# Zero-padded rows for the decay, rate and index products of a streaming encoder layer, whole modulation units, and a later load of constants

## The chip, the cores and the metric

The kernel runs on one core of one Trainium2 chip. The metric is device time in microseconds. Before the change it was 1761.67 us, the median of three runs (1757.67, 1761.67, 1761.89).

## The reference

One layer of a hybrid encoder for two groups of requests with the same weights: a prompt of 256 tokens, and 8 sample sequences of 16 tokens each with 256 cached tokens. The width is 1024.

```python
mod = silu(c) @ w_ada + b_ada                 # 6 x 1024 per sequence: shift1, scale1, gate1, shift2, scale2, gate2
h = rmsnorm(x) * (1 + scale1) + shift1
P = h @ w_in                                  # RWKV columns | attention and indexer | two branch gates
# branch A: RWKV-7 time mixing, 16 heads of 64
X = P + (P_prev - P) * mu                     # token shift; split r, k, v, wd (64), ad (64), gd
decay = exp(-exp(-softplus(-(w0 + tanh(wd) @ w_up)) - 0.5))
a = sigmoid(a0 + ad @ a_up)                   # rate
...                                           # state update per token, group norm, bonus, gate
# branch B: sparse attention, 16 heads of 64
score[t, s] = sum_h w[t, h] * relu(q_idx[t, h] . k_idx[s])     # 8 index heads of 64
...                                           # keep the best min(256, L/4) keys, softmax attention over them
m = sigmoid(gA) * (oA @ w_proj_a) + sigmoid(gB) * (oB @ w_proj_b)
x = x + gate1 * (m @ w_out)
x = x + gate2 * peer(rmsnorm(x) * (1 + scale2) + shift2)       # product-key mixture of 16384 experts
```

The outputs are the two results, the RWKV states, the last shifted rows and the new keys, values and index keys.

## The kernel before, in words

All 384 tokens (128 sample, 256 prompt) are handled together. A framework plans the program: it takes the instructions in the order in which the Python code makes them as their priority, simulates the engines, and lays down for each engine and for the SP queue (SyncE, which issues nearly all DMAs) a fixed order with waits. So engines work their queue in order, and a later edit can move instructions that it does not name. Memory comes from pools; a new tile waits until the tiles whose place it takes have been read for the last time.

`run` (L1590) has these stages:

- The front (to about 57 us): constants, the normalised input, the modulation units 0 to 7 that the first normalisation needs, and `rwkv_head` (L515), which makes the token-shifted low-rank inputs. `self.XW` holds 64 rows of decay input (after tanh) and 64 rows of rate input in one tile.
- The body (to about 692 us) works through `ORDER` (L177), one letter a unit: R is a pair of RWKV heads (`rwkv_pair`, L535), I the indexer (`index`, L890), the digits 1 to 3 the selection of keys, D a quarter of the attention (`dsa_quarter`, L932), G a gate unit, M a modulation unit from number 8 on (`mod_unit`, L383). Most of TensorE's work is three single-pass products of split (hi and lo) operands for each weight; weights arrive as 512 KB pieces through `raw` (L236), a ring of four buffers.
- The mix (`mix`, L1175) projects both branches, then the output projection, the expert scores, and the experts, which last to the end.

All products go through `mm` (L224). One on fewer than 128 rows (partitions of the operands) uses a part of the array; two on different row halves can be in it together. The places that matter here:

- `rwkv_pair`, L559 to L562: per pair of heads, the decay product takes rows 0 to 63 of `wup` and `XW`, the rate product rows 64 to 127, each of 384 columns.
- `index` (L912 to L930) makes the transposed indexer queries, `qiTs` for the sample (64 rows) and `qiTp` for the prompt (two heads one above the other, 64 rows each). `index_s` (L1015) multiplies them with the cached index keys `cki` (L1034, 64 rows of 256 columns, loaded by SP) and the new keys `kiT`; `index_p` (L983) multiplies one row half at a time. ACT applies the relu, and PE (sample) or DVE (prompt) adds up the heads.
- `mod_unit`: eight products of 32 output rows in four column groups of the array, four for each 512 KB half of the weight.
- `load_consts("clate", ...)`, L336: 200 KB of constants, used at L1203 and L1274 in the mix stage and by the experts' selection.

Of the kernel before, what the change touches and what calls it, by code (L numbers as in the profile page):

```python
# [17 lines left out]
AF = mybir.ActivationFunctionType  # L18
# [9 lines left out]
NT = 384  # L28
# [92 lines left out]
def layout(inp):  # L121
    f = {k: np.asarray(v) for k, v in inp.items()}
    A = {}

    def chunks(v):
        return v.reshape(-1, 128).T

    A["x"] = np.concatenate([f["x_sample"].reshape(128, 1024), f["x_prompt"].reshape(256, 1024)], 0)
    cc = np.concatenate([f["c_sample"], f["c_prompt"]], 0)
    A["cT"] = cc.T.reshape(8, 128, 9).transpose(1, 0, 2)  # L130
    A["w_ada"] = units256(f["w_ada"][0])
    A["b_ada"] = f["b_ada"]
    A["b_col"] = chunks(f["b_ada"][0, :2048])
    mu = np.zeros((27 * 128,), np.float32)
    mu[:RW] = f["mu_rw"][0]

    mu[RW:RW + 64] = np.tile(f["mu_rw"][0, RW - 32:], 2)
    sh = np.zeros((8, 27 * 128), np.float32)
    sh[:, :RW] = f["state_shift"][0]
    sh[:, RW:RW + 64] = np.tile(f["state_shift"][0, :, RW - 32:], 2)  # L140
    A["cols"] = np.concatenate([chunks(f["norm1_w"][0]), chunks(mu), chunks(f["w0"][0]), chunks(f["a0"][0]),
                                chunks(f["k_k"][0]), chunks(f["k_a"][0]), chunks(f["r_k"][0].reshape(-1)),
                                chunks(f["b_gate"][0])], 1)
    A["shT"] = sh.reshape(8, 27, 128).transpose(2, 0, 1)
    A["rows"] = np.concatenate([f["norm2_w"][0], f["lnx_w"][0], f["lnx_b"][0], f["b_gate"][0],
                                f["q_norm_w"][0], f["k_norm_w"][0]])[None]
    w3 = f["w_in"][0].reshape(8, 128, -1).transpose(1, 0, 2)
    A["w_in"] = np.concatenate([(np.tile(w3[:, :, c:c + 32], 3) if n == "wg" else w3[:, :, c:c + w]).reshape(128, -1)
                                for n, (c, w) in UNITS.items()], 1)
    A["wup2"] = np.concatenate([f["w_up"][0], f["a_up"][0]], 0)  # L150
    A["gup"] = np.concatenate([f["g_up"][0]] + 2 * [f["g_up"][0, 128:]], 0)
    for n in ("w_proj_a", "w_proj_b", "w_out", "w_pq"):
        A[n] = units256(f[n][0])
    A["keysT"] = f["peer_keys"][0].transpose(1, 3, 0, 2).reshape(128, 8, 128)
    A["puv"] = np.concatenate([f["peer_u"][0], f["peer_v"][0]], 1)
    A["pv"] = f["peer_v"][0]

    A["puT"] = f["peer_u"][0].reshape(128, 128, 8, 128).transpose(0, 3, 2, 1)

    A["cKT"] = f["cache_k"][0].reshape(4, 2, 256, 4, 2, 2, 64).transpose(3, 0, 5, 6, 1, 4, 2).reshape(4, 4, 128, 2, 2, 256)  # L160
    A["cV"] = f["cache_v"][0].reshape(4, 2, 2, 128, 4, 256).transpose(4, 0, 3, 1, 2, 5)
    A["cKI"] = f["cache_kidx"][0].transpose(2, 0, 1)
    A["S0"] = f["state_wkv"][0].reshape(8, 8, 2, 64, 64).transpose(2, 4, 1, 0, 3).reshape(128, 8, 8, 64)
    for n, (a, _) in PACKS.items():
        A[n] = a
    return {k: np.ascontiguousarray(v) for k, v in A.items()}
# [29 lines left out]
class K:  # L196
# [132 lines left out]
    def setup_front(self):  # L329
        nc = self.nc  # L330
        self.expb = self.fconst.tile([128, 8, 4, 16], BF16, name="expb")
        nc.vector.tensor_tensor(self.expb, self.c["blk"].unsqueeze(2).unsqueeze(3).to_broadcast([128, 8, 4, 16]),
                                self.c["dtt"].unsqueeze(1).unsqueeze(1).to_broadcast([128, 8, 4, 16]), op=OP.mult)
        rn = self.t([128, 128], tag="qkn")
        nc.sync.dma_start(rn, self.I["rows"][:, 5120:5248].to_broadcast([128, 128]))
        self.load_consts("clate", self.const)  # L336

        self.rt = self.fconst.tile([128, 3, 3, 4, 32], F32, name="rt")
        self.load_consts("crope", self.pool)
        rope = self.c["rope"]  # L340
        cos, sin = rope[:, :, 0], rope[:, :, 1]
        r = self.rt[:, 0]
        nc.gpsimd.tensor_copy(r[:, :, 0], cos)
        nc.gpsimd.tensor_copy(r[:, :, 1], cos)
        nc.gpsimd.tensor_scalar(r[:, :, 2], sin, -1.0, None, op0=OP.mult)
        nc.gpsimd.tensor_copy(r[:, :, 3], sin)
        for j in range(2):
            w1 = rn[:, 64 * j:64 * j + 32].unsqueeze(1).to_broadcast([128, 3, 32])
            w2 = rn[:, 64 * j + 32:64 * j + 64].unsqueeze(1).to_broadcast([128, 3, 32])
            r = self.rt[:, 1 + j]  # L350
            for m, w in enumerate((w1, w2, w2, w1)):
                nc.gpsimd.tensor_tensor(r[:, :, m], self.rt[:, 0, :, m], w, op=OP.mult)
        self.i64 = self.fconst.tile([128, 64], F32, name="i64")
        nc.vector.tensor_tensor(self.i64, self.ident[:, 0:64], self.ident[:, 64:128], op=OP.add)

        z = self.t([128, 520], tag="zero")
        nc.gpsimd.memset(z, 0.0)
        self.Bs, self.Bp, self.Bn = [], [], []
        for _ in range(2):
            b = self.dt_([64, 516])  # L360
            nc.sync.dma_start(b, z[:64, :516])
            self.Bs.append(b)
            for q in (self.Bp, self.Bn):
                b = self.dt_([64, 520])
                nc.sync.dma_start(b, z[:64])
                q.append(b)
# [16 lines left out]
    def mod_unit(self, u):  # L383

        nc = self.nc
        p = self.ps([128, 256], tag="mm")
        for h in range(2):
            w = self.raw(self.I["w_ada"][:, u, h * 4:h * 4 + 4])
            for g in range(4):
                self.mm(p[32 * g:32 * g + 32], self.st[:, h * 4 + g], w[:, g], start=(h == 0), stop=(h == 1), tp=(0, 32 * g))  # L390
        mr = self.t([128, 256], tag="mr", bufs=2, pool=self.fill)
        nc.scalar.activation(mr, p, AF.Copy)
        if u < 8:
            q = self.ps([128, 2, 9], tag="bx")
# [120 lines left out]
    def rwkv_head(self):  # L515
        nc = self.nc
# [5 lines left out]
        self.XW = self.shifted("wa", 24, "XW", 1)  # L522
        xv = self.shifted("wb", 25, "sig", 1)
        xg = self.shifted("wg", 26, "ra", 1)
        nc.scalar.activation(self.XW[0:64], self.XW[0:64], AF.Tanh)
        self.sigmoid(xv, xv)
        self.sigmoid(xg[:96], xg[:96])
        self.XV = [self.t([128, NT], F32R, tag=tag) for tag in ("XVh", "XVl")]
# [6 lines left out]
    def rwkv_pair(self, e):  # L535

        nc = self.nc
# [8 lines left out]
        wup = self.t([128, 128], tag="wup")  # L546
# [9 lines left out]
        nc.scalar.activation(gh[:96, 1], gup[:96, 1], AF.Copy)  # L556
        nc.vector.tensor_tensor(gh[64:96, 1], gup[64:96, 1], gh[64:96, 1], op=OP.subtract)
        sig, a, cs, Di, kk, sq = R("sig"), R("ra"), R("cs"), R("Di"), R("kk"), R("sq")
        for dst, rows, o in ((sig, 0, 0), (a, 64, 8)):  # L559
            p = self.ps([128, NT], tag="fx")  # L560
            self.mm(p, wup[rows:rows + 64], self.XW[rows:rows + 64])
            self.sigmoid(dst, p, self.hb[:, o + e:o + e + 1])  # L562
        nc.vector.tensor_tensor_scan(cs, self.c["scan"], sig, 0.0, op0=OP.mult, op1=OP.add)
        nc.vector.tensor_tensor(sig, cs, sig, op=OP.subtract)
# [325 lines left out]
    def index(self):  # L890
        nc = self.nc
# [17 lines left out]
        for i in range(3):  # L909
            nc.tensor.transpose(p[:, i], kr[:, i].rearrange("p a b -> p (a b)"), self.ident)  # L910
        nc.scalar.activation(kiT, p.rearrange("p i t -> p (i t)"), AF.Copy)
        qiTs = self.t([64, 8, 8, 16], tag="qiTs")  # L912
        qiTp = self.t([128, 4, 256], tag="qiTp")
        for u in range(2):
            x = self.t([128, 3, 256], tag="qx")
            self.nat3(f"qi{u}", x, 256)
# [2 lines left out]
            p = self.ps([128, 4, 128], tag="dx")  # L919
            for h in range(4):  # L920
                self.mm(p[:64, h], qr[:, 0, h], self.ident)
            nc.scalar.activation(qiTs[:, :, u * 4:u * 4 + 4].rearrange("p b h t -> p h b t"),
                                 p[:64].rearrange("p h (b t) -> p h b t", t=16), AF.Copy)
            p = self.ps([128, 2, 2, 128], tag="dx")
            for c in range(2):
                for i in range(2):
                    nc.tensor.transpose(p[:, c, i], qr[:, 1 + i, 2 * c:2 * c + 2].rearrange("p a b -> p (a b)"), self.ident)
            nc.scalar.activation(qiTp[:, u * 2:u * 2 + 2], p.rearrange("p c i t -> p c (i t)"), AF.Copy)
        self.index_s(qiTs, kiT, wi[:, 0])
        self.index_p(qiTp, kiT, wi)  # L930

# [51 lines left out]
    def index_p(self, qiT, kiT, wi):  # L983
        nc = self.nc
        for i in range(2):
# [1 line left out]
            sc = self.iscp[:, 128 * i:128 * i + n]  # L987
            self.isc.append(sc)
            for par in range(2):
                pr = slice(64 * par, 64 * par + 64)  # L990
                for c0 in range(0, 4, 2):
                    p = self.ps([128, 2, 256], tag="dx")
                    for j in range(2):
                        self.mm(p[:, j, :n], qiT[pr, c0 + j, i * 128:(i + 1) * 128], kiT[pr, 128:128 + n], tp=(64 * par, 0))
                    for j in range(2):
                        h = 2 * (c0 + j) + par
                        w = wi[:, 1 + i, h:h + 1]
# [17 lines left out]
    def index_s(self, qiT, kiT, wi):  # L1015
# [15 lines left out]
        for b in range(8):  # L1031
            p = self.ps([128, 272], tag="dx")
            q = qiT[:, b].rearrange("p h t -> p (h t)")
            cki = self.t([64, 256], tag="cki", bufs=2)  # L1034
            with self.tc.issue_after(self.wdma.ins):
                nc.sync.dma_start(cki, self.I["cKI"][:, b])
            self.mm(p[:, 0:256], q, cki)
            self.mm(p[:, 256:272], q, kiT[0:64, b * 16:b * 16 + 16])
            rl = self.t([128, 272], tag="rel", bufs=2)
            nc.scalar.activation(rl, p, AF.Relu)  # L1040
            self.mm(psc, LW[:, b].rearrange("p a b -> p (a b)"), rl, start=(b == 0), stop=(b == 7))
# [548 lines left out]
    def run(self):  # L1590
        hs = self.ctx.enter_context(ExitStack())
        self.halves = self.open(hs, "halves")
        with ExitStack() as front:
# [41 lines left out]
                self.nc.sync.dma_start(self.O["sh"], self.last)  # L1635
            fh.close()
            self.hpool2 = self.open(self.ctx, "hpool2", side="right")
            qs = self.ctx.enter_context(ExitStack())
            self.qpool = self.open(qs, "qpool", side="right")
            with ExitStack() as s:  # L1640
# [114 lines left out]
```

## Time and profile before

| what | value |
|---|---|
| median of 3 runs | 1761.67 us |
| the profiled execution's own time | 1759.49 us |
| its span, first to last instruction | 1757.7 us |
| mean granted TensorE clock | 0.981 |
| bytes read, written in HBM | 403.23 MB, 31.30 MB |

The profile is one execution. PE is TensorE's products, PEld its weight loads, DVE VectorE, ACT ScalarE, POOL GpSimd, SPq the queue of SyncE. A row of a timeline has the start, the length from the first to the last instruction of the row, the engine, the line, the operands as output<-inputs with their shapes, and how many instructions were merged; in square brackets stands the idle time before it and what ended that. A product in full fp32 shows as two instructions, and products are pipelined: the spacing of starts, not the length, is what each costs TensorE. A row by operands has the count, the busy time and the mean length in ns. A row of a tile has the smallest, median and largest length in ns and the first and last start in us.

### The profile page before, as it was taken

What the parts mean: (1) busy time and instruction counts of PE and PEld (TensorE: products, weight loads), DVE (VectorE), ACT (ScalarE), POOL (GpSimd) and SP (SyncE); (2) the same over time, 40 slices, a digit from 0 to 9 for tenths busy, and PEclk for the clock granted to TensorE, in tenths of its full rate; (3) what the DMA queues carried; (4) which work ended last, traced back from release to release, by engine and by line L of the source; (5) the groups of instructions that cost most, each with busy time, mean ns of one, the idle gap of its engine ahead of it and who ended that gap; (6) DMA issues with size and microseconds to landing.
All of it is one profiled execution on the core that took longest, in us unless ns stands there. A gap on an engine that the chain in (4) does not pass through costs nothing.

```text
span 1757.7 us, 33129 instructions
## 1 busy us (share of the span) xinstructions
PE 1679.5 (96%) x12392; PEld 1410.2 (80%) x12392; DVE 1353.6 (77%) x2907; ACT 747.5 (43%) x1666; POOL 550.5 (31%) x616
## 2 busy tenths in 40 slices
PE   6999899999999999999998999999999999999998
PEld 4988788777888877899887889999976667767766
DVE  4448878778867765556999998899957778778787
ACT  4533343334342333335323255578853433443344
POOL 2433343333333421024032233342243224323232
PEclk8999899999999999999999999999999999999999
DMA  8543662555365365765488999997569999999996
GB/s 305 161 123 101 187 194 68 145 166 174 94 197 161 94 207 189 246 193 171 144 334 313 358 333 366 397 340 238 179 251 381 348 346 376 375 349 391 349 379 216
DMA packets 172537, 436.71 MB, mean 248 GB/s; under 512 B 46036, under 2 KB 86100, under 8 KB 155992
## 3 DMA queue, kind: packets, MB, share of 16 engines
q1 hardware_dynamic: 153944, 300.36, 50.8%
q0 software_dynamic: 18432, 134.23, 19.7%
q8 instruction: 98, 1.61, 0.4%
q14 instruction: 63, 0.52, 0.1%
HBM read 403.23 MB, written 31.30 MB: 247 GB/s over the span
## 4 chain that ended last, share of the span: by engine, by line
PE 55%; DVE 19%; DMA 11%; issue 8%; ACT 3%; POOL 2%; SPq 1%; DVEq 0%; POOLq 0%; ACTq 0%
PE mm L226 21%; PE fx L226 10%; PE dx L226 10%; PE cp L226 6%; PE bx L226 6%; DMA raw<-in_puv,pe 3%; DVE wl L234 3%; DVE raw L1580 2%; DVE acc L1586 2%; DMA w<-in_puT 2%; DMA w<-in_pv 2%; ACT wh L230 1%; DMA w<-in_w_in 1%; DVE TX L698 1%; DMA NL<-d 1%
## 5 line engine op out<-in xcount | busy, mean ns | idle before, releaser
L234 DVE TENSOR_TENSOR wl<-w,wh 128x1024 fp32r<-128x1024 f32 (+1 forms) x276 | 345.8, 1260 | 109.0 <-ACT wh L230 71.3
L230 ACT ACTIVATE wh<-w 128x1024 fp32r<-128x1024 f32 (+1 forms) x284 | 296.6, 1050 | 163.7 <-PE mm L226 74.3
L1573 POOL DMA_INDIRECT raw<-in_puv,pe x128 | 173.6, 1356 | 423.4 <-PE dx L226 155.4
L226 PE MATMUL fx<-h2h,wl 128*128 128x256 f32 x704 | 200.1, 285 | 8.2 <-DVE wl L234 8.0
L226 PE MATMUL fx<-h2h,wh 128*128 128x256 f32 x704 | 200.6, 285 | 1.4 <-ACT wh L230 1.1
L226 PE MATMUL fx<-h2l,wh 128*128 128x256 f32 x704 | 197.4, 281 | 0.0
L1586 DVE SCALAR_TENSOR_TENSOR acc<-raw,dots,acc 128x1024 f32<-128x1024 f32 x127 | 166.1, 1308 | 14.8 <-ACT dots L1582 14.8
L1580 DVE SCALAR_TENSOR_TENSOR raw<-raw,sh 128x1024 f32<-128x1024 f32 x128 | 158.9, 1241 | 14.0 <-DMA raw<-in_puv,pe 13.8
L226 PEld LDWEIGHTS fx<-h2h,wl 128*128 128x128 f32 x704 | 132.7, 189 | 12.3 <-DVE wl L234 11.5
L226 PEld LDWEIGHTS fx<-h2h,wh 128*128 128x128 f32 x704 | 132.6, 188 | 6.4 <-ACT wh L230 3.6
L226 PEld LDWEIGHTS fx<-h2l,wh 128*128 128x128 f32 x704 | 132.9, 189 | 1.6 <-issue 1.1
L226 PE MATMUL mm<-LTh,wh 128*128 128x384 f32 (+2 forms) x352 | 123.4, 351 | 1.4 <-ACT wh L230 0.8
L226 PE MATMUL mm<-LTl,wh 128*128 128x384 f32 (+2 forms) x352 | 123.1, 350 | 0.9 <-POOL LTl L488 0.9
L226 PE MATMUL mm<-LTh,wl 128*128 128x384 f32 (+2 forms) x352 | 122.4, 348 | 0.0
L226 PE MATMUL mm<-h2f,w 128*128 128x256 f32 x448 | 104.0, 385 | 0.0
L226 PE MATMUL mm<-wh,LTh 128*128 128x256 f32 x336 | 100.3, 299 | 2.9 <-ACT qx L888 2.9
L1581 ACT ACTIVATE dots<-dots 128x1 f32<-128x1 f32 x128 | 25.6, 200 | 177.0 <-DVE raw L1580 176.5
L226 PE MATMUL mm<-wl,LTh 128*128 128x256 f32 x336 | 99.4, 296 | 0.0
L226 PE MATMUL mm<-wh,LTl 128*128 128x256 f32 x336 | 98.6, 293 | 0.0
L226 PEld LDWEIGHTS mm<-h2f,w 128*128 128x128 f32 x448 | 85.0, 192 | 12.2 <-issue 0.2
L226 PE MATMUL fx<-h2f,w 128*128 128x256 f32 x320 | 73.8, 383 | 0.0
L226 PEld LDWEIGHTS mm<-LTh,wh 128*128 128x128 f32 (+2 forms) x352 | 66.5, 189 | 7.1 <-issue 3.0
(577 smaller groups left out, 4235.0 us busy)
## 6 DMA issues: line engine op xcount, KB each, us to landing
w<-in_puT SPq DMA_DIRECT2D x128, 512.0 KB, 7.1
w<-in_pv SPq DMA_DIRECT2D x128, 512.0 KB, 6.6
w<-in_w_in SPq DMA_DIRECT2D x70, 512.0 KB, 4.5
w<-in_w_ada SPq DMA_DIRECT2D x48, 512.0 KB, 4.8
cKT<-in_cKT SPq DMA_DIRECT2D x32, 256.0 KB, 4.3
cV<-in_cV SPq DMA_DIRECT2D x32, 256.0 KB, 4.5
w<-in_w_pq SPq DMA_DIRECT2D x16, 512.0 KB, 4.2
d<-wst SPq DMA_DIRECT2D x8, 832.0 KB, 4.3
```

The lines of the kernel that those rows point to most:

```text
L226: return self.nc.tensor.matmul(out, l, r, start=start, stop=stop, skip_group_check=True, **kw)
L230: self.nc.scalar.activation(hi, src, AF.Copy)
L234: (self.nc.vector if eng == "v" else self.nc.gpsimd).tensor_tensor(lo, src, hi, op=OP.subtract)
L698: nc.vector.tensor_tensor(X[:, :t, :t], T[:, :t, :t].rearrange("p s c -> p c s"), NL[:, :t, t].unsqueeze(1).to_broadcast([48, t, t]), op=O ...
L1573: d = nc.gpsimd.indirect_dma_start(out=bass.AP(tensor=u.tensor, offset=u.offset, ap=[u.ap[0], [1, 2048]]), out_offset=None, in_=self.I["puv"],
L1580: nc.vector.scalar_tensor_tensor(u, u, 1.0, h2, op0=OP.mult, op1=OP.mult, accum_out=dot)
L1581: nc.scalar.activation(dot, dot, AF.Gelu_apprx_tanh)
L1586: nc.vector.scalar_tensor_tensor(acc, v, dot, acc, op0=OP.mult, op1=OP.add)
```

## The change

- The decay input goes into a tile of its own, `XD`, whose rows 64 to 127 are cleared; rows 0 to 63 of `XW` are cleared after the tanh has read them. Both products then use all 128 rows of `wup`.
- The sample's indexer queries get 64 more rows of zeros and the cached index keys are stored twice, one above the other; the prompt's indexer queries become two tiles with the other half cleared, so each evacuation is split in two. All index products use 128 rows.
- `mod_unit` asks for both halves of its weight ahead of the products; for units 8 and up the products of the second half come first.
- The constants `clate` are loaded after the body's pools are closed, into the pool `hpool2`.

```diff
-    A["cKI"] = f["cache_kidx"][0].transpose(2, 0, 1)
+    A["cKI"] = np.concatenate(2 * [f["cache_kidx"][0].transpose(2, 0, 1)], 0)
...
-        self.load_consts("clate", self.const)
-
...
-        for h in range(2):
-            w = self.raw(self.I["w_ada"][:, u, h * 4:h * 4 + 4])
+        w = [self.raw(self.I["w_ada"][:, u, h * 4:h * 4 + 4]) for h in range(2)]
+        first = 0 if u < 8 else 1
+        for h in (first, 1 - first):
             for g in range(4):
-                self.mm(p[32 * g:32 * g + 32], self.st[:, h * 4 + g], w[:, g], start=(h == 0), stop=(h == 1), tp=(0, 32 * g))
+                self.mm(p[32 * g:32 * g + 32], self.st[:, h * 4 + g], w[h][:, g], start=(h == first), stop=(h != first), tp=(0, 32 * g))
...
-        nc.scalar.activation(self.XW[0:64], self.XW[0:64], AF.Tanh)
+        self.XD = self.t([128, NT], tag="XD")
+        nc.gpsimd.memset(self.XD[64:128], 0.0)
+        nc.scalar.activation(self.XD[0:64], self.XW[0:64], AF.Tanh)
+        nc.gpsimd.memset(self.XW[0:64], 0.0)
...
-        for dst, rows, o in ((sig, 0, 0), (a, 64, 8)):
+        for dst, src, o in ((sig, self.XD, 0), (a, self.XW, 8)):
             p = self.ps([128, NT], tag="fx")
-            self.mm(p, wup[rows:rows + 64], self.XW[rows:rows + 64])
+            self.mm(p, wup, src)
...
-        qiTs = self.t([64, 8, 8, 16], tag="qiTs")
-        qiTp = self.t([128, 4, 256], tag="qiTp")
+        qiTs = self.t([128, 8, 8, 16], tag="qiTs")
+        nc.gpsimd.memset(qiTs[64:128], 0.0)
+        qiTp = self.t([128, 2, 4, 256], tag="qiTp")
+        for par in range(2):
+            nc.gpsimd.memset(qiTp[64 - 64 * par:128 - 64 * par, par], 0.0)
...
-            nc.scalar.activation(qiTp[:, u * 2:u * 2 + 2], p.rearrange("p c i t -> p c (i t)"), AF.Copy)
+            for par in range(2):
+                pr = slice(64 * par, 64 * par + 64)
+                nc.scalar.activation(qiTp[pr, par, u * 2:u * 2 + 2], p[pr].rearrange("p c i t -> p c (i t)"), AF.Copy)
...
-                        self.mm(p[:, j, :n], qiT[pr, c0 + j, i * 128:(i + 1) * 128], kiT[pr, 128:128 + n], tp=(64 * par, 0))
+                        self.mm(p[:, j, :n], qiT[:, par, c0 + j, i * 128:(i + 1) * 128], kiT[:, 128:128 + n])
...
-            cki = self.t([64, 256], tag="cki", bufs=2)
+            cki = self.t([128, 256], tag="cki", bufs=2)
...
-            self.mm(p[:, 256:272], q, kiT[0:64, b * 16:b * 16 + 16])
+            self.mm(p[:, 256:272], q, kiT[:, b * 16:b * 16 + 16])
...
             self.hpool2 = self.open(self.ctx, "hpool2", side="right")
+            self.load_consts("clate", self.hpool2)
```

More of the change, by code (lines that the diff above doesn't have):

```diff
@@ L921, in index @@
                 self.mm(p[:64, h], qr[:, 0, h], self.ident)
-            nc.scalar.activation(qiTs[:, :, u * 4:u * 4 + 4].rearrange("p b h t -> p h b t"),
+            nc.scalar.activation(qiTs[0:64, :, u * 4:u * 4 + 4].rearrange("p b h t -> p h b t"),
                                  p[:64].rearrange("p h (b t) -> p h b t", t=16), AF.Copy)
@@ L989, in index_p @@
             for par in range(2):
-                pr = slice(64 * par, 64 * par + 64)
                 for c0 in range(0, 4, 2):
```

## Prediction

> **What bounds the kernel now.** I read the page's busy times and the chain that ended last, then a table of stages, then TensorE's timeline at each place that the diff touches, and at the end the DMA queue around the mix.
>
> ```profile
> PE 1679.5 (96%) x12392; PEld 1410.2 (80%) x12392; DVE 1353.6 (77%) x2907; ACT 747.5 (43%) x1666; POOL 550.5 (31%) x616
> ```
> ```profile
> PE 55%; DVE 19%; DMA 11%; issue 8%; ACT 3%; POOL 2%; SPq 1%; DVEq 0%; POOLq 0%; ACTq 0%
> ```
>
> TensorE (PE) is busy 96% of the span and carries 55% of the chain. Everything the change touches lies before about 725 us, so the stages there decide. In the next table the columns are the stretch, its length, and then PE, weight loads, DVE, ACT and POOL with counts, the granted clock, the DMA share and GB/s.
>
> ```profile
> 135.00:150.00 15.00, 15.00 (x80) 12.61 (x79) 14.41 (x38) 6.04 (x17) 4.20 (x13) 1.00 0.25 72
> ```
> ```profile
> 154.00:198.00 44.00, 37.63 (x309) 33.78 (x308) 38.07 (x124) 13.43 (x28) 17.99 (x18) 0.96 0.37 104
> 198.00:300.00 102.00, 101.83 (x1057) 82.77 (x1056) 80.42 (x221) 40.66 (x99) 31.17 (x61) 0.97 0.58 171
> ```
> ```profile
> 300.00:450.00 150.00, 144.09 (x1648) 120.18 (x1648) 116.21 (x310) 51.44 (x127) 54.88 (x86) 0.98 0.50 145
> 450.00:600.00 150.00, 146.79 (x1626) 125.16 (x1625) 117.63 (x299) 56.64 (x136) 57.30 (x80) 0.99 0.48 146
> 600.00:692.00 92.00, 87.68 (x1120) 72.71 (x1119) 60.15 (x157) 31.62 (x70) 18.76 (x16) 1.00 0.59 192
> ```
>
> From 198 to 692 PE is idle 0.17 + 5.91 + 3.21 + 4.32 = 13.6 of 494 us: it is the bound, and PE time saved there should show at the end. From 154 to 198 it is not: PE idles 6.4 of 44 us and DVE works 38.07 of 44. That DVE stretch begins earlier: from 135 to 150 DVE is busy 14.41 of 15, with the selection of keys that starts when the sample scores of the indexer are ready.
>
> What does a product on half the rows cost PE? Three places of its timeline (start, us, line, operands, count), and the plain rate at the end:
>
> ```profile
> 57.42 0.34 PE L226 MATMUL mm<-LTl,wh 128*128 128x384 f32 x1
> 57.60 0.34 PE L226 MATMUL mm<-LTh,wl 128*128 128x384 f32 x1
> 57.87 0.92 PE L226 MATMUL fx<-XW,wup 64*128 64x384 f32 x4
> 58.71 0.44 PE L226 MATMUL mm<-LTh,wh 128*128 128x384 f32 x1
> ```
> ```profile
> 141.94 0.34 PE L226 MATMUL mm<-LTl,wh 128*128 128x384 f32 x1
> 142.21 1.13 PE L226 MATMUL dx<-kiT,qiTp 64*128 64x256 f32 x4
> 143.27 0.44 PE L226 MATMUL mm<-LTh,wl 128*128 128x384 f32 x1
> ```
> ```profile
> 296.27 0.28 PE L226 MATMUL mm<-wh,LTh 128*128 128x256 f32 x1
> 296.48 0.91 PE L226 MATMUL fx<-XW,wup 64*128 64x384 f32 x2
> 297.32 0.39 PE L226 MATMUL mm<-wl,LTh 128*128 128x256 f32 x1
> ```
> ```profile
> 962.51 3.62 PE L226 MATMUL mm<-h2f,w 128*128 128x256 f32 x16
> 965.97 3.62 PE L226 MATMUL fx<-h2f,w 128*128 128x256 f32 x16
> ```
>
> An fp32 product shows as two instructions. Full height, they follow each other every (965.97 - 962.51)/16 = 0.216 us at 256 columns, so 0.324 at 384. The neighbours' normal step at 384 columns is 57.60 - 57.42, about 0.17. Before the 64-row products the step is 57.87 - 57.60 = 0.27: entering another tile shape costs 0.10, and leaving it costs as much again.
>
> **Index products.** These 64-row groups exist between 105 and 154 us:
>
> ```profile
> L226 PE MATMUL dx<-cki,qiTs 64*128 64x256 f32 x16 | 5.5, 427 | 0.0
> ...
> L226 PE MATMUL dx<-kiT,qiTp 64*128 64x256 f32 x16 | 4.5, 402 | 0.0
> L226 PE MATMUL dx<-kiT,qiTp 64*128 64x128 f32 x16 | 2.8, 296 | 0.0
> ...
> L226 PE MATMUL dx<-kiT,qiTs 64*128 64x16 f32 x16 | 2.5, 231 | 0.0
> ```
>
> The prompt's scores (index_p) come in eight visits of four instructions. The visit at 142.21 takes 143.27 - 141.94 - 0.17 = 1.16 us from the stream; four full-height instructions take 0.864. Saved: 0.29 a visit, 2.3 in all. The sample's scores (index_s) come in eight iterations, nine visits, where the two switches save at least 0.19: 1.8. Together 4.1 us of PE. I let the 1.8 pass, because the selection on DVE starts from those scores; of the 2.3 I let only 0.5 pass, since it is saved while DVE works 14.41 of 15 us and just ahead of a stage where PE idles 6.4. Value -2.3; ends 0 (all of it becomes idle time before 198) and -4.1.
>
> **Decay and rate.** One product each per pair of heads, eight pairs:
>
> ```profile
> L226 PE MATMUL fx<-XW,wup x32: 482/535/587, 57.9 to 574.9; 64*128 64x384 f32 x32
> ```
>
> Here height was used. At 57.87 both products, on rows 0 to 63 and 64 to 127, ran together: 58.71 - 57.60 - 0.17 = 0.94 us for both, where two full-height ones take 4 x 0.324 = 1.30. That is +0.36. At 296.48 the decay ran alone: 297.32 - 296.27 less a 256-column step of about 0.12 is 0.93, and its partner cost as much, so full height saves 1.86 - 1.30 = 0.56 there. In the timeline five of the eight pairs run together, one runs together in part (taken as 0), two run apart. Three of the five, and both of those apart, have another small-tile group beside them, so a switch of 0.10 stays: 5 x 0.36 + 0.4 - 2 x 0.56 + 0.2 = +1.3 us. Ends: -1 (it depends on how the new order would have paired them) and +3.
>
> The Trainium skill, TensorE: Matmul & The Clock Gate, Part 3, speaks against this edit: small products in different row groups run concurrently, so a pair lasts about as long as one. By it the two would have cost 0.65 and the loss would be 0.65 a pair, 5.2 in all. The trace has the concurrency but also the 0.20 of switches, and not in every pair.
>
> The clears on POOL and the tanh into a new tile come once, ahead of the first use at 57.87, under the stream of products that runs there; uncovered I would count 1 us for them (an estimate, two instructions of the 0.59 us that an ACT copy takes further down).
>
> **Modulation units.** Units 0 to 7 keep their order. For 8 to 23 the half that is loaded last now goes first, so eight products become ready at once:
>
> ```profile
> 427.53 1.07 PE L226 MATMUL mm<-w,cst 128*32 128x256 f32 x16
> 428.53 0.44 PE L226 MATMUL cp<-S,TT 64*64 64x128 f32 x4
> ```
> ```profile
> 551.65 0.34 PE L226 MATMUL mm<-LTh,wl 128*128 128x384 f32 x1
> 551.92 0.64 PE L226 MATMUL mm<-w,cst 128*32 128x256 f32 x8
> 552.49 0.33 PE L226 MATMUL cp<-cQ,bn 64*64 64x64 f32 x4
> ```
> ```profile
> 500.22 0.63 PE L226 MATMUL mm<-w,cst 128*32 128x256 f32 x4
> 500.78 0.92 PE L226 MATMUL fx<-XW,wup 64*128 64x384 f32 x4
> ```
> ```profile
> 643.67 0.64 PE L226 MATMUL mm<-w,cst 128*32 128x256 f32 x8 [2.19 <-DMA w<-in_w_ada]
> ```
>
> A whole unit costs 428.53 - 427.53 = 1.00 with the way out and 1.10 with the way in; a half alone costs 552.49 - 551.65 - 0.17 = 0.67, two of them 1.34. Joining saves 0.24. In the timeline the sixteen units lie in 26 runs, but only four units are cut at the half; the other cuts fall where the planner put a more urgent group between (the last four instructions of one unit, at 500.22, cost 0.56 with the way out although they are a quarter of it). The edit removes the first sort: 4 x 0.24 = -0.9. If all cuts went it would be 2.4 by joined halves and, counting groups of four that are cut through, up to about 5.6. The added wait: PE takes its queue in order, so behind a unit that waits for its second half stand all later products. One such wait is there already, 2.19 us at 643.67 for a first half. Since the planner can now place the unit later, I take 0, ends -2 and +2. Both halves hold two of the four stream buffers a little longer; the SP queue issues them side by side already.
>
> **Late constants and small things.**
>
> ```profile
> L297 SPq DMA_DIRECT2D clate<-in_clate x1: 432/432/432, 34.5 to 34.5; - x1
> ```
> ```profile
> 703.78 0.80 SPq L1171 DMA_DIRECT2D px<-d  x2
> ```
> ```profile
> 718.12 0.38 SPq L974 DMA_DIRECT2D d<-qr  x1
> ```
> ```profile
> 723.08 0.35 SPq L1271 DMA_DIRECT2D keysT<-in_keysT  x1
> ```
> ```profile
> L928 ACT ACTIVATE qiTp<-dx x2: 580/589/598, 86.4 to 98.4; 128x512 f32<-128x512 f32 x2
> ```
>
> The one load leaves SP at 34.5 us, where PE has full input soon after: 0. It returns in memory that the attention pool gives up, in a queue with the loads px of the mix at 703.78, which feed the first projection. Costs 0.43 us of SP's issue; taken as 0, with an upper end in the third rival. The split evacuation of the indexer queries adds two ACT instructions of 0.59 us where the table has ACT 6.04 of 15 us busy; the clears of the padded halves are three more POOL instructions, with POOL 4.20 of 15 busy; the cached indexer keys move twice the rows in each of eight loads, with DMA 0.25 busy. Nobody on the path waits for these: the first scores stand behind products of other units in PE's queue. All lie under PE's stream: 0; uncovered about 1. The readers of the late constants (L1203 on ACT, L1274 on DVE) are moved behind the later landing; work behind them in those two queues would wait only if the planner misjudges the landing, which is in the third rival.
>
> **Sum.** -2.3 + 1.3 - 0.9 + 0 = -1.9 us, on the profiled execution's 1759.49 (span 1757.7). The median of the runs shown, 1761.67, lies 2.2 above that; I put the difference on the median: 1759.8. About 0.3%, or 5.3 us, is what a measurement can tell from no change.
>
> **Rivals.** First, faster: all PE savings pass and nearly all cuts of the modulation units go: -4.1 + 1.3 - 5.6 = -8.4, so 1753.3. For it: PE is the bound from 198 on, and a unit that is ready at once gives the planner fewer reasons to cut. Against: the DVE stretch before 198, and cuts by urgent groups that the diff does not touch. It decides if the 26 runs become 16 or 17.
>
> Second, no gain: two 64-row products that run together take as long as one (4 x 0.324 / 2 = 0.65), and if the new neighbours would have hidden the switches anyway, the loss is 8 x 0.65 = +5.2 in place of +1.3; with the other terms +2.0, so 1763.7. For it the five pairs that ran together; against it the two switches of 0.10 that they paid, and the pairs that ran apart. It decides if decay and rate are found between other small-tile groups in most pairs. The rule of the Trainium skill cited above gives the same.
>
> Third, slower: the load of the late constants stands in SP's queue ahead of px, and waits for memory that the attention still uses. keysT at 723.08 shows such a wait, for the write d<-qr issued at 718.12. If the constants' place is freed only then, px goes from 703.78 to about 722, and the projection with it; PE has some attention work to fill, so I count 14 of the 18 us: -1.9 + 14 = +12, so 1774. It decides if px is issued after about 711. Against it: the planner knows when the place comes free, and the new tile is smaller and elsewhere than keysT.
>
> **Chances.** The forecast 0.48 (0.38 within 0.3%, 0.08 faster, 0.02 slower, since the whole plan is drawn anew); first rival 0.30 (0.28 faster, 0.02 same); second 0.10 (0.09 same, 0.01 slower); third 0.12 (slower). So faster 0.36, same 0.49, slower 0.15. The range runs from a little under the first rival to 1768, leaving out most of the third: 1750 to 1768.
>
> **What would show it.** Right: no 64-row products of wup, cki or kiT; index visits with plain steps of 0.216 at 256 columns; decay and rate at 1.3 us a pair; fewer than 26 runs of the modulation units, none cut at eight with both halves late; px still near 704. Wrong: PE's idle time between 154 and 198 falling to nothing (then the index gain passed whole), or a wait of SP ahead of px, or longer waits of PE for in_w_ada than 2.19.

## The result and the profile after

| | before | after |
|---|---|---|
| median of 6 runs each, us | 1763.74 (1757.67 to 1768.56) | 1751.45 (1748.10 to 1756.19) |
| ratio to before, 95% interval | | 0.9930 [0.9905, 0.9954] |
| the profiled execution's own time, us | 1759.49 | 1749.86 |
| its span, us | 1757.7 | 1748.1 |

The kernel became 12.3 us faster, 0.7%, more than the 0.3% that a measurement can tell. The forecast was 1759.8, a change of less than those 0.3%; the range of 1750 to 1768 holds the result, but the likeliest case did not come. Of all the runs in this text one, of e9, was slow (2702.89 us at a granted clock of 0.555), and the ratio of e9 leaves it out.

The page of the changed kernel, busy times and the chain by engine:

```profile
PE 1673.2 (96%) x12392; PEld 1410.4 (81%) x12392; DVE 1356.0 (78%) x2907; ACT 749.5 (43%) x1668; POOL 556.0 (32%) x621
```
```profile
PE 61%; DVE 18%; DMA 11%; issue 5%; ACT 3%; POOL 2%; SPq 0%; DVEq 0%; POOLq 0%; ACTq 0%
```

PE has as many instructions as before and 6.3 us less busy time; the share of the chain in which an engine waits for nothing that the profile shows ("issue") fell from 8% to 5%.

Where the time went is read by setting the same events side by side. The first product of the split inputs starts 1.3 us later than before (37.2 against 35.9), the last index product starts at 148.9 instead of 153.1, the first product of the mix starts at 699.3 instead of 708.1, and from there to the end both kernels take the same to within 1 us. So all of the gain lies in the body. This row spans the body from its first transposes of keys to the mix, first of before, then of after (columns as in the prediction: stretch, length, PE, weight loads, DVE, ACT, POOL with counts, granted clock, DMA share, GB/s):

```profile
70.10:708.10 638.00, 613.83 (x6310) 518.10 (x6309) 463.41 (x1205) 231.92 (x547) 213.14 (x311) 0.98 0.49 149
```
```profile
71.20:699.30 628.10, 609.63 (x6311) 520.68 (x6309) 462.74 (x1206) 232.75 (x547) 208.15 (x311) 0.98 0.50 152
```

The body is 9.9 us shorter: 4.2 of PE's busy time and 5.7 of its idle time (638.0 - 613.8 = 24.2 before, 18.5 after), with the same products and the same work on DVE and ACT.

The stages of after that answer to those of the prediction, each moved by what lies ahead of it:

```profile
131.00:146.00 15.00, 15.00 (x90) 14.69 (x90) 12.88 (x35) 6.00 (x17) 5.78 (x12) 1.00 0.22 63
150.00:194.00 44.00, 38.52 (x303) 34.30 (x303) 39.10 (x126) 13.55 (x28) 19.52 (x21) 0.92 0.39 114
194.00:300.00 106.00, 105.73 (x1094) 86.51 (x1095) 85.07 (x232) 43.07 (x104) 30.42 (x61) 0.97 0.55 166
300.00:450.00 150.00, 147.65 (x1700) 124.31 (x1698) 121.49 (x318) 50.68 (x127) 59.62 (x91) 0.99 0.49 149
450.00:600.00 150.00, 149.88 (x1654) 127.84 (x1651) 114.22 (x289) 56.90 (x136) 51.81 (x78) 1.00 0.49 149
600.00:692.00 92.00, 84.20 (x1034) 68.27 (x1032) 57.90 (x158) 31.86 (x76) 14.31 (x13) 0.96 0.62 197
```

Two things are to be seen. PE's idle time ahead of the attention, 44.00 - 38.52 = 5.5 us, is still there (6.4 before): the index gain did not turn into idle time. And in the two middle stages PE's idle time fell from 5.91 + 3.21 us to 2.35 + 0.12, which the prediction had not forecast. In the last stage it grew from 4.32 to 7.80, as that fixed window now ends 9 us nearer to the mix.

The wait that closes the first of these stages stood at 197.75 in before and stands at 193.97 in after, just as long. Timeline of PE, idle time and what ended it in square brackets, before and then after:

```profile
197.75 0.85 PE L959 MATMUL dx<-cfirst,qr 128*128 128x128 f32 x6 [3.41 <-DVE qr L881]
```
```profile
193.97 0.85 PE L966 MATMUL dx<-cfirst,qr 128*128 128x128 f32 x6 [3.41 <-DVE qr L883]
```

A visit of the prompt's index products in after, in PE's timeline, and the two rows of before that follow the visit which the prediction showed:

```profile
139.05 0.34 PE L226 MATMUL mm<-LTl,wh 128*128 128x384 f32 x1
139.23 1.03 PE L226 MATMUL dx<-kiT,qiTp 128*128 128x256 f32 x4
139.90 0.53 PE L226 MATMUL mm<-LTh,wl 128*128 128x384 f32 x1
140.27 0.34 PE L226 MATMUL mm<-LTh,wh 128*128 128x384 f32 x1
140.45 0.34 PE L226 MATMUL mm<-LTl,wh 128*128 128x384 f32 x1
```
```profile
143.55 0.34 PE L226 MATMUL mm<-LTh,wh 128*128 128x384 f32 x1
143.72 0.34 PE L226 MATMUL mm<-LTl,wh 128*128 128x384 f32 x1
```

From the last product ahead of the visit to the second one behind it, after takes 140.45 - 139.05 = 1.40 us and before 143.72 - 141.94 = 1.78. The visit saves 0.38, not 0.29. The difference is the step from 143.27 to 143.55: the first full-height product behind the small group took 0.28 us instead of the plain 0.17. That step recurs in the body of before and after alike (36 and 25 places of 384 columns, median 0.28; at 256 columns 27 and 26 places, 0.22 instead of 0.12). A visit of the 64-row form so costs four things of about 0.10 us: the way in (0.27 instead of 0.17), the first of its four instructions (0.32, where the next two take 0.216), the way out, and the first product behind it. Together that is about 0.39 us.

Decay and rate of the first pair of heads in after:

```profile
58.70 0.81 PE L226 MATMUL fx<-XD,wup 128*128 128x384 f32 x2
59.34 0.81 PE L226 MATMUL fx<-XW,wup 128*128 128x384 f32 x2
59.70 0.63 PE L226 MATMUL mm<-LTh,wh 128*128 128x384 f32 x1
60.17 0.34 PE L226 MATMUL mm<-LTl,wh 128*128 128x384 f32 x1
```

From 58.70 to 60.17, less the plain step of the one product between, they cost 1.30 us, as forecast. The queue of SP at the mix, and the wait of the constants' load there:

```profile
694.97 0.80 SPq L1177 DMA_DIRECT2D px<-d  x2
...
708.53 0.38 SPq L981 DMA_DIRECT2D d<-qr  x1
...
714.53 0.36 SPq L297 DMA_DIRECT2D clate<-in_clate  x1
```
```profile
SPq L297 <- DMA d<-qr: 3.7, 1, 3.7
```

The late constants wait for the landing of the attention's last write, as the third rival said, but the first loads of px stand 20 us ahead of them, and from the mix to the end after takes no longer than before (1048.8 us against 1049.6).

### The profile page after: what moved, and what is told of

Its sections match the earlier page's. It is cut to its first block, busy times and chain, and to the rows that moved or that the text cites. A ratio compares the mean times of both kernels' runs of the same rounds, so it can differ in the third digit from the quotient of the medians.

```text
span 1748.1 us, 33136 instructions
## 1 busy us (share of the span) xinstructions
PE 1673.2 (96%) x12392; PEld 1410.4 (81%) x12392; DVE 1356.0 (78%) x2907; ACT 749.5 (43%) x1668; POOL 556.0 (32%) x621
## 4 chain that ended last, share of the span: by engine, by line
PE 61%; DVE 18%; DMA 11%; issue 5%; ACT 3%; POOL 2%; SPq 0%; DVEq 0%; POOLq 0%; ACTq 0%
PE mm L226 24%; PE fx L226 11%; PE dx L226 11%; PE cp L226 7%; PE bx L226 6%; DMA w<-in_pv 3%; DVE raw L1586 3%; DVE wl L234 3%; DVE acc L1592 3%; DMA raw<-in_puv,pe 2%; DMA w<-in_puT 1%; ACT wh L230 1%; DMA w<-in_w_in 1%; DMA w<-in_w_ada 1%; DVE psi L1321 1%
## 5 line engine op out<-in xcount | busy, mean ns | idle before, releaser
L1586 DVE SCALAR_TENSOR_TENSOR raw<-raw,sh 128x1024 f32<-128x1024 f32 x128 | 158.6, 1239 | 12.3 <-DMA raw<-in_puv,pe 12.2
```

The source lines that it names most:

```text
L1586: nc.vector.scalar_tensor_tensor(u, u, 1.0, h2, op0=OP.mult, op1=OP.mult, accum_out=dot)
```

## The experiments

Three theories stand in the expectations. S: each small-tile group that disappears from the stream saves its switches on PE, and all of that shows at the end. D: the index saving is mostly taken up by DVE ahead of the attention, as the prediction had it. P: not the shapes but the order that the planner draws anew makes the difference. Times are medians; ratios are to before, timed beside it. The medians of before were 1764.46 us for e1 to e4, 1764.50 for e5 to e8 and 1765.24 for e9 to e12.

**e1, after once more, and e2, after with 64-row index products.** In e2 everything of the change stays except that the products read rows 0 to 63 (or one half) of the padded tiles:

```diff
-  self.mm(p[:, j, :n], qiT[:, par, c0 + j, ...], kiT[:, 128:128 + n])
+  self.mm(p[:, j, :n], qiT[64 * par:64 * par + 64, par, c0 + j, ...], kiT[64 * par:64 * par + 64, 128:128 + n], tp=(64 * par, 0))
...
-  q = qiT[:, b].rearrange("p h t -> p (h t)")
+  q = qiT[0:64, b].rearrange("p h t -> p (h t)")
...
-  self.mm(p[:, 0:256], q, cki)
+  self.mm(p[:, 0:256], q, cki[0:64])
-  self.mm(p[:, 256:272], q, kiT[:, b * 16:b * 16 + 16])
+  self.mm(p[:, 256:272], q, kiT[0:64, b * 16:b * 16 + 16])
```

> The changed kernel itself, as the base for the runs beside it on the same chip. Both theories: about 12 us below the kernel before (0.993), as measured; the spread shows how far chips and rounds differ.

> The changed kernel, but the index products read only the 64 rows that hold data, as before; every engine's order is the same as in the changed kernel. Theory S (shapes: TensorE is the bound through the whole body, so its saved switches show in full): 4.1 us slower than the changed kernel, and the start of the mix later by as much. Theory D (the one of the prediction: DVE is the bound up to 198 us and swallows most): 2.3 us slower or less. Theory P (the gain is the new plan of the order, not the shapes): no difference over 1 us.

Measured: e1 1754.07, 0.9925 [0.9906, 0.9944]; e2 1759.43, 0.9969 [0.9946, 0.9992]. The order of instructions on each engine is the same in both, so P has nothing to say here. The shape alone is worth 5.4 us by medians and 7.8 by the ratios, with some 5 us of room either way: by the timed runs D's bound of 2.3 is only just ruled out, and S's 4.1 is not exceeded beyond doubt. The traces are sharper. The stage from the first split product to the last index product takes 111.5 us in e1 and 117.6 in e2 (before 117.2, after 111.7), the body 629.5 and 635.0. And the index groups themselves, each from the last product ahead of it to the second behind it, add up to 5.2 us more in e2.

The visit in e2, again with the long first product behind it (145.16 to 145.44):

```profile
144.10 1.13 PE L226 MATMUL dx<-kiT,qiTp 64*128 64x256 f32 x4
145.16 0.44 PE L226 MATMUL mm<-LTh,wl 128*128 128x384 f32 x1
145.44 0.34 PE L226 MATMUL mm<-LTh,wh 128*128 128x384 f32 x1
```

Why did DVE, busy 14.41 of 15 us here in before, not take up the saving? Between the first and the last step of the sample's selection DVE does the same instructions in e1 and e2. The stretch in e1, in e2 and in before, and then the waits of DVE for PE in e2:

```profile
135.70:158.00 22.30, 22.30 (x150) 21.44 (x149) 22.30 (x63) 8.79 (x23) 10.76 (x23) 1.00 0.26 74
```
```profile
137.10:161.90 24.80, 24.80 (x150) 21.07 (x149) 23.02 (x62) 8.69 (x23) 9.16 (x23) 1.00 0.25 73
```
```profile
135.20:160.00 24.80, 24.80 (x150) 21.12 (x149) 23.00 (x62) 8.68 (x23) 9.14 (x23) 1.00 0.26 74
```
```profile
DVE bon L600 <- PE fx L226: 0.9, 1, 0.9
DVE wl L234 <- PE mm L226: 0.3, 1, 0.3
DVE MBs L618 <- PE fx L226: 0.3, 1, 0.3
DVE MBp L627 <- PE fx L226: 0.2, 1, 0.2
```

PE does the same 150 instructions in 22.3 us in the one and in 24.8 in the other, and DVE, nearly full, still waits 1.7 us for products of PE in e2 and not at all in e1 or after. The trace of before has the same four waits with the same lengths in the same 24.8 us. DVE was paced by PE, by four short waits that a busy share of over 90% hides; they are 1.7 of the 2.5 us, and the rest is DVE's own busy time, 0.7 us less in e1. D falls. But the room is used up: in e1 DVE is busy for all of the 22.30 us, so a further saving of PE in this stretch might well stop there (no run tries it).

**e3, the index part alone on before** (the lines of the diff for `cKI`, `qiTs`, `qiTp`, `cki` and the index products, nothing else).

```diff
-  qiTs = self.t([64, 8, 8, 16], tag="qiTs")
-  qiTp = self.t([128, 4, 256], tag="qiTp")
+  qiTs = self.t([128, 8, 8, 16], tag="qiTs")
...
+  qiTp = self.t([128, 2, 4, 256], tag="qiTp")
```

> The kernel before with the index part of the change alone (padded queries, doubled keys, split evacuation). Theory S: 4 us faster than before, within some 3 us that the redrawn order can give or take. Theory D: 2 us faster or less. Theory P: anything between 5 us faster and 5 us slower, without relation to the 4.1.

Measured: 1759.07, 0.9970 [0.9952, 0.9988]: -5.4 us by medians, the same as e2 gives from the other side, in an order practically that of before (33 of PE's 12392 places differ).

**e4, the late constants alone, and e6, they and the decay and rate products on full height.** (Decay and rate alone do not fit in memory while the constants stay where they were, so that part was not run by itself.)

```diff
-        self.load_consts("clate", self.const)
...
             self.hpool2 = self.open(self.ctx, "hpool2", side="right")
+            self.load_consts("clate", self.hpool2)
```

> The kernel before with the late load of the constants alone; no product changes, but the planner draws the order anew. Theory S: no difference over 2 us, and as many changes of tile shape as before. Theory P: a difference of several us to either side, with TensorE's idle time and half-clock time in the body changed by as much.

> The kernel before with full-height decay and rate products and the late constants (the one needs the room of the other). To be read against the run with the late constants alone, where all eight pairs ran together. Theory S with the concurrency of the pairs counted: 8 x (1.30 - 1.04) = 2 us slower than that run, plus 0.1 to 0.2 for each pair that stood beside other small groups. Theory P: several us away from it, either way, with idle and half-clock time to match.

Measured: e4 1769.29, 1.0023 [1.0003, 1.0044]; e6 1765.85, 1.0014 [0.9996, 1.0032]. In e4 px is again ahead of the constants by 19 us, so the loss of 4.8 us by medians, whose interval begins at 1.0003, is no wait at the mix: in the profiled execution the body itself is longer. Its row, beside that of before above:

```profile
71.50:718.40 646.90, 620.52 (x6310) 526.05 (x6308) 462.07 (x1206) 231.08 (x545) 204.35 (x311) 0.97 0.49 147
```

The order of the body was drawn anew, and in this one the granted clock is at half for 44.4 us of the body, against 28.1 in before. e6 adds the full-height decay and rate to that and comes out 0.0009 of the time lower, with intervals that overlap: the price of that part could not be told from nothing. The two orders also part from 183 us on, so this is no test of the form alone.

**e5, the modulation part alone on before, and e7, after without it.**

```diff
-        for h in range(2):
-            w = self.raw(self.I["w_ada"][:, u, h * 4:h * 4 + 4])
+        w = [self.raw(self.I["w_ada"][:, u, h * 4:h * 4 + 4]) for h in range(2)]
+        first = 0 if u < 8 else 1
+        for h in (first, 1 - first):
...
```

> The kernel before with the modulation part alone (both halves asked for first, last half first from unit 8 on). A change of tile shape costs about 0.3 us in all (0.09 in, 0.09 out, 0.10 on the first product after), so four units joined are worth 4 x 0.34. Theory S: 1.4 us faster, with 22 runs of these units in place of 26. Theory P (a redrawn order moves idle time and half-clock time): a difference of 3 us or more to either side that the count of runs does not explain.

> The changed kernel with the modulation units as before. Theory S: 1.4 us slower than the changed kernel, with four more runs of these units. Theory P: 3 us or more to either side. If the modulation part were the main gain beside the index part, 5 us slower.

Measured: e5 1755.89, 0.9962 [0.9945, 0.9979]; e7 1759.41, 0.9981 [0.9964, 0.9997]. The part is worth 6.7 us alone and, by the ratios of e7 and e1, 0.0056 of the time or 9.9 us (with 4.4 of room) when taken out: several times what S gave it. And not by joined halves. Counted so that any other product between ends a run, the sixteen units lie in 29 runs in before (the prediction and the expectations have 26), 28 in e5, 26 in e7 and 22 in after. What changed in e5 is the order of other work: the 64x64 products of the RWKV heads lie in 112 groups instead of 123. That count does not explain the part either: after has 120 of these groups and e7, without the part, 119.

**e8, after with the decay and rate products back on 64 rows.**

```diff
-        for dst, src, o in ((sig, self.XD, 0), (a, self.XW, 8)):
+        for dst, src, rows, o in ((sig, self.XD, 0, 0), (a, self.XW, 64, 8)):
...
-            self.mm(p, wup, src)
+            self.mm(p, wup[rows:rows + 64], src[rows:rows + 64])
```

> The changed kernel, but decay and rate read only the 64 rows that hold data, each its own row half, so that they can run together again. Theory S with concurrency: 2 us faster than the changed kernel if all pairs run together (1.04 in place of 1.30 each), 6 us slower if all run apart (2.06). Theory P: a difference that follows idle and half-clock time.

Measured: 1764.89, 1.0013 [0.9996, 1.0029], about 15 us slower than after. Hardly any of this is the price of the 64-row form: five of the eight pairs run together in e8 and three apart, which by 1.04 and 2.06 us against 1.30 makes about 1 us. The order differs from the second pair of heads on. To the end of the index products e8 takes the same 111.5 us as e1; the loss comes later, with PE idle in gaps of over 0.5 us for 22.9 us of the body instead of 16.7. The 64-row form in the same order is not among the runs, so this part is not tried by itself.

**e9, the index and modulation parts without the other two.**

```diff
         self.load_consts("clate", self.const)
...
         for dst, rows, o in ((sig, 0, 0), (a, 64, 8)):
             p = self.ps([128, NT], tag="fx")
             self.mm(p, wup[rows:rows + 64], self.XW[rows:rows + 64])
```

(These lines stay as in before; the index and modulation lines are those of after.)

> The kernel before with the index and the modulation parts, without the full-height decay and rate and without the late constants. Alone they gave 0.997 and 0.9962. If the two add up and the other two parts bring nothing of their own: 0.993, 12 us faster than before, as fast as the changed kernel. If full-height decay and rate are needed for the gain: some 5 us slower than the changed kernel.

Measured: 1751.09, 0.9918 [0.9896, 0.9940]. The whole gain is there without the decay, rate and late-constant edits. It cannot be told from after (0.9930, 0.9925), so it is no better version either. On PE its order is that of e5 but for 24 places among the index products, so the two show the index part a third time: 4.8 us by medians, 7.8 by the ratios.

**e10, both halves asked for first, but the first half's products still first.** Shown against e5:

```diff
-        first = 0 if u < 8 else 1
+        first = 0
```

> The kernel before with only the first half of the modulation part: both halves are asked for ahead of the products, and the products keep their order. TensorE's order stays nearly that of before. Theories S and P: no difference over 2 us. If the early request for the second half were what the modulation part gains by: 6 us faster.

Measured: 1762.37, 0.9992 [0.9965, 1.0019], with nearly the order of before on PE (8 places differ). The early request alone brings nothing that can be told, though 6 us lies just inside the end of the interval; what moves the time in e5 is most likely that the second half goes first, and so when the planner can place the unit.

**e11 and e12, edits that should mean nothing but a new order:** the late constants loaded behind `rwkv_head` into the same pool, and the rotary table loaded earlier.

```diff
-        self.load_consts("clate", self.const)
...
                 self.rwkv_head()
+                self.load_consts("clate", self.const)
```
```diff
-        self.load_consts("crope", self.pool)
...
                 self.front_h()
...
+                self.load_consts("crope", self.pool)
```

> The kernel before with the 200 KB of late constants loaded some us later in the front, after the low-rank inputs; no product, evacuation or other load changes, but the planner draws another order of the body. Theory S: within 2 us of before. Theory P: several us away from it, either way, with TensorE's idle and half-clock time in the body to match.

> The kernel before with the rotary table (96 KB) loaded ahead of the first weights of the body in place of behind them; no product changes, and the planner draws a third order. Theory S: within 2 us of before. Theory P: several us away from it, either way.

Measured: e11 1768.05, 1.0004 [0.9982, 1.0027]; e12 1765.83, 1.0007 [0.9985, 1.0029]. e11 kept the order of before in the body after all, so it says only how well two like kernels agree. e12 did get a new order, much like that of e4 (PE has other work in 1016 of 12392 places), and no change of time. So no edit that only redraws the order shows a clear cost: e4's 4 us are hardly clear of noise.

**What the orders have in common.** For the body of all fourteen profiled executions I counted, from the trace of PE, how often the shape of the tile changes from one product to the next, the sum of PE's gaps over 0.5 us, and the time at which the granted clock was at half:

| kernel | body, us | changes of shape | idle, us | half clock, us |
|---|---|---|---|---|
| before | 638.0 | 419 | 20.4 | 28.1 |
| e3 index alone | 633.7 | 388 | 23.0 | 22.8 |
| e4 constants alone | 646.9 | 417 | 22.5 | 44.4 |
| e5 modulation alone | 634.3 | 403 | 19.9 | 25.9 |
| e6 constants, decay, rate | 641.5 | 408 | 17.2 | 38.2 |
| e7 after without modulation | 632.9 | 377 | 18.2 | 30.7 |
| e8 after, 64-row decay and rate | 640.8 | 388 | 22.9 | 30.7 |
| e9 index and modulation | 630.6 | 372 | 19.8 | 29.1 |
| e10 early request | 640.8 | 419 | 21.5 | 34.1 |
| e11 | 639.3 | 419 | 21.6 | 24.0 |
| e12 | 639.3 | 415 | 22.3 | 27.3 |
| after | 628.1 | 376 | 16.7 | 23.9 |
| e1 after again | 629.5 | 376 | 17.4 | 23.9 |
| e2 after, 64-row index | 635.0 | 405 | 18.4 | 20.5 |

The least-squares fit is body = 552.6 + 0.148 x changes + 0.64 x idle + 0.41 x half clock, with all kernels within 2.1 us but e8 (3.3); the standard errors of the three prices are 0.03, 0.24 and 0.08. A group is two changes, so 0.30 us, near the 0.29 to 0.39 that the index groups differ by between e2 and e1. Between before and after it puts 43 x 0.148 = 6.4 us on the changes of shape, 3.7 x 0.64 = 2.4 on idle time and 4.2 x 0.41 = 1.7 on the clock, 10.5 together for the 9.9 seen. Of the changes of shape the index part takes away 31 by itself (e3) and the modulation part 16 (e5). It is a fit of four numbers to fourteen executions, a ledger and not a proof; the price of a change of shape is what e2 and the timeline show by themselves. The clock above all is not the order's: before, e10 and e11, with nearly one order, have 28.1, 34.1 and 24.0 us at half clock, a wider spread than the 4.2 between before and after.

The Trainium skill, TensorEngine Tiling (Array Packing), Tiling Modes, says that changing the tiling mode drains TensorE and gives no figure. The traces show a cost at such changes, by the fit about 0.15 us each; that it is a drain no run here shows.

## Why the prediction was right or wrong

**Right.** No 64-row products of `wup`, `cki` or `kiT` are left. Decay and rate cost 1.30 us for the pair shown. px went first (694.97), so the third rival did not come, though the wait on which it rested did: 3.7 us for d<-qr. The small edits of the front cost nothing that can be told: the stream starts 1.3 us later, and the first key transposes start at 71.2 in after and at 73.4 in e1, which is the same kernel. That the range held the time was luck as far as the forecast goes: it reached to the first rival, 1753.3, and the sum behind the forecast gave 1.9 of the 12.3 us.

**Wrong: "of the 2.3 I let only 0.5 pass, since it is saved while DVE works 14.41 of 15 us and just ahead of a stage where PE idles 6.4".** All of it passed, and more. e2, with every engine's order that of e1, loses 5.4 us. The step that failed is the reading of DVE's busy share as a bound. DVE began with the index products of PE and waited for PE four times within the stretch; when PE was quicker DVE did the same selection in 22.3 us instead of 24.8, and the PE idle time of 3.41 us behind it moved earlier by 3.8 us unshortened. The table of windows could not tell this. The waits of DVE in that stretch, which were there in before, name who was late, and the prediction did not ask for them. Its sign of being wrong, PE's idle time from 154 to 198 falling to nothing, was wrong with it: the gain passed whole with 5.5 of those 6.4 us still there.

**Mis-sized: the index term, 4.1 us.** It was 5.5 (117.2 to 111.7 for the stage). "Entering another tile shape costs 0.10, and leaving it costs as much again" left out the first product behind the group, 0.28 instead of 0.17. (What it put down to leaving is in part the slower first instruction of the group; its total of 1.16 us for the visit had that in it.) With the product behind, the eight prompt visits save 0.38 each, 3.0, and nine sample visits 0.19 + 0.10 each, 2.6: 5.6. The rows were there: in the quoted visits the product behind the group shows 0.44 where its neighbours show 0.34, and its next start was one row further down.

**Wrong: "4 x 0.24 = -0.9" for the modulation units.** e5 measured -6.7 [-9.7, -3.7]. Joined halves had nearly no part (29 runs to 28). The prediction priced the edit by the products that it names; what it moved was the place of everything else, which the prediction had only as "0.08 faster, 0.02 slower, since the whole plan is drawn anew". The ledger explains e5's body: 16 changes fewer give 2.4, idle 0.3 and clock 0.9, 3.6 together for 3.7 seen. The timed runs show 6.7. Part of the gap is which execution was profiled: that of before took 1759.49 us, where its runs beside e5 have a median of 1764.50, and e10 and e11, with nearly its order, have bodies of 640.8 and 639.3, 5.0 to 6.5 longer than e5's. Taking the part out of after costs 9.9, of which the body's rows show 3.4 to 4.8, and there the changes of shape, 377 against 376, have no share. That a unit whose halves are both there before it starts leaves the planner better orders is argued, not shown; e10 shows only that the early request is hardly it. The time that the units hold their accumulators, from the first product to the end of the evacuation, is 54.6 us in all in before, 64.9 in e5, 49.8 in after. It goes the wrong way in e5, so that is not the reason. Why this order is the better one beyond the counts stays open.

**Undecided: "+1.3" for decay and rate.** e9 has the gain of after without them and without the late constants, so both edits together are worth about nothing, within some 5 us (the half widths of e9 and e1, 3.9 and 3.4, taken together). e6 against e4 says -1.6, with about as much room. The second rival's loss of 5.2 for the lost concurrency does not show: e6 against e4 rules it out, with the orders different, and e9 against after does not quite. The term itself has the fault of the index term: to the second product behind the group, the pair at 57.87 takes 58.99 - 57.60 less two plain steps, 1.04 us, and two apart 2.06, so the prediction's own sum becomes 5 x 0.26 + 0.4 - 2 x 0.76 + 0.2 = +0.4. The Trainium skill, TensorE: Matmul & The Clock Gate, Part 3, says that small products in different row groups run concurrently. The traces agree for five of the eight pairs of before, but such a pair takes 1.04 us with its switches where one full-height product takes 0.65, so full height loses 0.26 us a pair there and not 0.65.

**The first rival** had the direction and nearly the size for a wrong reason: it wanted 26 runs to become 16 or 17, and they became 22. That is luck. The right sum by the measured parts is -5.4 (e3) - 6.7 (e5) = -12.1 for a measured -12.3, with the other two at about zero; with some 3 us of room on each part the close fit is partly chance. The sum on record was -1.9.

The wait of PE for a modulation weight, by which the prediction would have been wrong upward, did grow, in one place:

```profile
636.18 1.94 PE L226 MATMUL mm<-w,cst 128*32 128x256 f32 x16 [3.11 <-DMA w<-in_w_ada]
```

The longest such wait is 3.11 instead of 2.19 us, and the gaps elsewhere shrank by more.

## What to carry to other kernels

Where one engine is full and its neighbour nearly so, a busy share does not say who paces whom: ask for the waits of the neighbour in that stretch before writing a saving off. Price a group of another tile shape by the distance from the last plain product ahead of it to the second plain product behind it, and count groups rather than products. Where a planner draws the order, an edit of dependences moves work that it does not name; give such an edit a wide term of its own (here from nothing in e12 to +4 us, hardly clear of noise, in e4 and -7 in e5), and settle it by running the part alone and by taking it out.

## What the runs showed of the hardware

- A full-height product behind a small-tile group takes 0.28 us instead of 0.17 at 384 columns and 0.22 instead of 0.12 at 256. Entering and leaving cost 0.09 to 0.10 each, and the first instruction of a 64-row fp32 group as much again: 0.39 us in all for a visit of the prompt's index products.
- In the body of after the granted clock goes to half four times, for 3.4 or 6.8 us, each time around a stall of PE: from 195.1 to 201.9, just behind the stall that ends at 193.97, and from 635.4, at the wait that ends at 636.18. Not every stall does it: 0.80 us at 619.3 did not. So an idle gap can cost more than its length: the fit has 0.41 us for each us at half clock.
- With the same products (before, e4, e5, e10, e11, e12) the body had between 24.0 and 44.4 us at half clock and between 19.9 and 22.5 us of gaps; with nearly the same order too (before, e10, e11), 24.0 to 34.1 and 20.4 to 21.6.
